# A hybrid prefix-flow block on one core: the softplus of the state space's steps moved ahead of the gated recurrence, two gate panels split ahead of the state space

## The chip, the core and the metric

One Trainium2 chip; the program runs on one of its cores. The time is device microseconds of one execution. Of the kernel before three executions were timed: 3110.61, 3120.03 and 3121.97 us, median 3120.03. A further execution was profiled, and all rows below are of that one.

The engines are named as in the profile: PE is TensorE (PEld its weight loads), DVE is VectorE, ACT is ScalarE, POOL is GpSimd, SP is SyncE, which issues most DMAs.

## The reference, cut to what matters

The block mixes tokens in four branches, gates the branches and sends the result through grouped experts. What this change touches is the fourth branch, a state space (Mamba-like) with a step `dt` per token, direction and head:

```
dt = jax.nn.softplus(dt_raw.reshape(bsz, t_len, 2, H_D) + lp['ssm_dt_bias'])
log_a = dt * (-jnp.exp(lp['ssm_A_log']))[:, None, :, None]
y_f, s_mf = chunk_scan(ch, bh * dt[0][..., None], xh, log_a[0][..., None], s_mf)
y_r, s_mb = chunk_scan(flip_t(ch), flip_t(bh * dt[1][..., None]), flip_t(xh), flip_t(log_a[1][..., None]), s_mb)
...
gates = jax.nn.sigmoid(gate_raw.reshape(bsz, t_len, N_BRANCH, D_MODEL))
merged = gates[:, :, 0] * (branches[0] @ lp['w_branch'][0])
```

The second branch is a gated recurrence (hgrn) over 2048 tokens plus 256 of context, in both directions. The gates are 32 column panels of 128, a matrix product of all tokens with a 1024 x 4096 part of `w_in`.

## The kernel before, in words

All large products run as three float32r products: a weight panel of 128 x 1024 is loaded (`wraw`), cast by ACT to its rounded part (`whi`, L1294), and the rest (`wlo`) is found by a subtraction on DVE or POOL (L1295); this is what "split" means. `wpanel` (L1428) does it, `fetch` (L1420) issues the load. The tokens' rounded part and rest are kept in SBUF (`hb0h`, `hb0l`, `hb1h`, `hb1l`), and `mm3` (L1434) issues the three products (L1438 to L1440) for each of 8 slices of 128, 24 matmuls of 128x512 for one block of 512 tokens.

The order of the program: the projections that hgrn needs for the second half of the tokens (`hgrn_cols(1)`, L1555: four f panels, `token_major` for V and dt_raw, and the panels q0, q1, g0, g1); `hgrn` (L28); the other projections of that half (`other_cols(1)`, L1557); the state space (`ssm`, L182); a convolution branch; a Fourier branch (`fft`); then the gates (L1593), two blocks of tokens for each panel, whose results go to DRAM (`GS`, L1598); then the branch products.

The engines do not follow that order. A scheduler of the framework lays down, before the run, one queue for each engine: an instruction that is ready goes first if it is earlier in the program, and later ones fill the gaps. On the chip each queue is then served in that order. Tiles of one tag are handed out in program order, as their buffers come free; a pool that is opened later uses the memory of one that was closed, and its tiles wait until the older tiles there are done with. Three consequences for what follows:

- PE's gate products fill the gaps of hgrn, of the state space and of the Fourier branch. They go panel by panel, in program order, with 3 PSUM buffers of tag "mm".
- Every third panel (2, 5, 8, ...) keeps its `whi` and `wlo` in the pool `wx` (one buffer), which lies in memory that hgrn's last tiles hold; the others use the ring `wring` (two buffers each). All `wraw` loads share two buffers. Before the change an odd panel's subtraction runs on POOL, an even one's on DVE; the loads of these panels are issued from the POOL queue.
- The first part of the state space (pool `sd`, L193) lies partly in hgrn's memory. So it starts when hgrn ends, though its input dt_raw (`dtr`, written at L1465) is complete long before.

Hgrn (L28) first passes over all tokens for the states (`state_pass`, L72: long runs of small DVE instructions, L85 and L42), then, for each of 4 segments and 2 pairs of heads, goes through 7 levels (L128 to L147: a copy on ACT, 16 matmuls, L137, two masked copies and two products on DVE), and ends with a norm: square on ACT (L168), a matmul (L170), square root on ACT (L172), then on DVE reciprocal (L173), product (L174) and the result `hy` (L176).

The state space (L182) takes the softplus of `dtr` plus its bias (L201 to L214): Exp on ACT (L204), a reciprocal, and a polynomial in a loop of 8 (L211, L212), on DVE, each instruction on 128 x 144 values. It is computed without a Ln. Then `na` = -exp(A_log) (L216, L217), `la` = dt * na (L219), transposes of `la` on PE (L229), ten copies to `R` (L230), a scan over 16 places for each direction (L234), sums over blocks (L241 to L250), Exp on ACT (L251, L252), transposes back (L269). In its second part come the convolution (L279 to L300: three DVE instructions, L289 to L291, for each piece) and the scans over chunks.

Of the kernel before, what the change touches and what calls it, by code (L numbers as in the profile page):

```python
# [4 lines left out]
F32 = mybir.dt.float32  # L5
# [3 lines left out]
AF = mybir.ActivationFunctionType  # L9
OP = mybir.AluOpType  # L10
# [168 lines left out]

def ssm(G, tc, dtr, XR, ZT, XC, XB, cumD, ecumD, elD, SBd, YT):  # L182


    nc = tc.nc
    NCH = TA // 64
    with tc.tile_pool(reuse_waits="tile", name="sst", bufs=1) as st:

        dtm = st.tile([128, 18, 8], F32, name="dtm")
        cumc = st.tile([128, 18, 4, 4], F32, name="cumc")  # L190
        dtw = st.tile([128, 18, 8], F32, name="dtw")
        elB = st.tile([128, NCH, 4], F32, name="elB")
        with tc.tile_pool(reuse_waits="tile", name="sd", bufs=1) as dp:  # L193
            f = [128, 18, 8]
            x = dp.tile(f, F32, name="dx")
            u = dp.tile(f, F32, name="du")
            s = dp.tile(f, F32, name="ds_")
            s2 = dp.tile(f, F32, name="ds2")
            ac = dp.tile(f, F32, name="dac")
            bc = lambda t: t.unsqueeze(1).to_broadcast(f)  # L200
            nc.vector.tensor_tensor(x, dtr, bc(G.dtb), op=OP.add)  # L201
            nc.vector.tensor_scalar(u, x, -1.0, None, op0=OP.mult)
            nc.vector.tensor_tensor(u, u, x, op=OP.min)
            nc.scalar.activation(u, u, AF.Exp)  # L204
            nc.vector.tensor_scalar(s, u, 2.0, None, op0=OP.add)
            nc.vector.reciprocal(s, s)
            nc.vector.tensor_mul(s, s, u)
            nc.vector.tensor_mul(s2, s, s)
            nc.vector.tensor_scalar(ac, s2, 2.0 / 19, 2.0 / 17, op0=OP.mult, op1=OP.add)
            for k in (15, 13, 11, 9, 7, 5, 3, 1):  # L210
                nc.vector.tensor_mul(ac, ac, s2)  # L211
                nc.vector.tensor_scalar(ac, ac, 2.0 / k, None, op0=OP.add)  # L212
            nc.vector.tensor_mul(ac, ac, s)
            nc.vector.scalar_tensor_tensor(dtm, x, 0.0, ac, op0=OP.max, op1=OP.add)  # L214
            na = dp.tile([128, 8], F32, name="na")
            nc.scalar.activation(na, G.alog, AF.Exp)  # L216
            nc.vector.tensor_scalar(na, na, -1.0, None, op0=OP.mult)  # L217
            la = dp.tile(f, F32, name="la")
            nc.vector.tensor_tensor(la, dtm, bc(na), op=OP.mult)  # L219
            R = dp.tile([128, TA], F32, name="R")  # L220
            E = dp.tile([128, TA], F32, name="E")
            nc.gpsimd.memset(R, 0.0)
            for d in range(2):
                p0 = 32 * d
                for i0 in range(0, 18, 4):
                    k = min(4, 18 - i0)
                    pt = G.psum("tr")
                    for i in range(k):
                        nc.tensor.transpose(pt[0:4, i * 128:i * 128 + 128], la[:, i0 + i, d * 4:d * 4 + 4], G.ident)  # L229
                    nc.vector.tensor_copy(R[p0:p0 + 4, i0 * 128:(i0 + k) * 128], pt[0:4, :k * 128])  # L230
                r = R[p0:p0 + 4].rearrange("p (b j) -> p b j", j=16)
                for j in range(1, 16):
                    a, b = (j, j - 1) if d == 0 else (15 - j, 16 - j)
                    nc.vector.tensor_add(r[:, :, a], r[:, :, a], r[:, :, b])  # L234
                rc = R[p0:p0 + 4].rearrange("p (c b j) -> p c b j", b=4, j=16)
                ex = dp.tile([128, NCH, 3], F32, name="ex", bufs=2)
                e = ex[p0:p0 + 4]
                lastj = 15 if d == 0 else 0
                blk = (0, 1, 2) if d == 0 else (3, 2, 1)
                pos = (0, 1, 2) if d == 0 else (2, 1, 0)  # L240
                nc.vector.tensor_copy(e[:, :, pos[0]], rc[:, :, blk[0], lastj])  # L241
                for i in (1, 2):
                    nc.vector.tensor_add(e[:, :, pos[i]], e[:, :, pos[i - 1]], rc[:, :, blk[i], lastj])
                o = 1 - d
                nc.vector.tensor_add(rc[:, :, o:o + 3, :], rc[:, :, o:o + 3, :],
                                     e.unsqueeze(3).to_broadcast([4, NCH, 3, 16]))
                ch = R[p0:p0 + 4].rearrange("p (c j) -> p c j", j=64)
                last = ch[:, :, 63 if d == 0 else 0]
                w = R[p0 + 64:p0 + 68].rearrange("p (c j) -> p c j", j=64)
                nc.vector.tensor_tensor(w, last.unsqueeze(2).to_broadcast([4, NCH, 64]), ch, op=OP.subtract)  # L250
                nc.scalar.activation(R[p0 + 64:p0 + 68], R[p0 + 64:p0 + 68], AF.Exp)  # L251
                nc.scalar.activation(E[p0:p0 + 4], R[p0:p0 + 4], AF.Exp)  # L252
                el = dp.tile([128, NCH], F32, name="el", bufs=2)
                nc.vector.tensor_copy(el[p0:p0 + 4], E[p0:p0 + 4].rearrange("p (c j) -> p c j", j=64)
                                      [:, :, 63 if d == 0 else 0])
                for c2 in range(2):
                    nc.sync.dma_start(cumD[c2, d * 4:d * 4 + 4], ch.rearrange("p (i c) j -> p i c j", c=2)[:, :, c2])
                nc.sync.dma_start(ecumD[d * 4:d * 4 + 4], E[p0:p0 + 4])
                nc.sync.dma_start(elD[d * 4:d * 4 + 4], el[p0:p0 + 4])
                lb = elD[d * 4:d * 4 + 4]  # L260
                elt = dp.tile([128, 4, NCH], F32, name="elt")
                nc.sync.dma_start(elt[d * 64:d * 64 + 64],
                                  bass.AP(tensor=lb.tensor, offset=lb.offset, ap=[[0, 64], [NCH, 4], [1, NCH]]))
                nc.vector.tensor_copy(elB[d * 64:d * 64 + 64], elt[d * 64:d * 64 + 64].rearrange("p h c -> p c h"))
            for i0 in range(0, 18, 4):
                k = min(4, 18 - i0)
                pt = G.psum("tr")
                for i in range(k):
                    nc.tensor.transpose(pt[:, i * 128:i * 128 + 128], R[:, (i0 + i) * 128:(i0 + i + 1) * 128], G.ident)  # L269
                nc.vector.tensor_copy(cumc[:, i0:i0 + k], pt[:, :k * 128].rearrange("p (i q x) -> p i q x", q=4, x=32)  # L270
                                      [:, :, :, 0:4])
            nc.vector.tensor_mul(dtw, dtm, cumc[:, :, 2:4, :].rearrange("p i q h -> p i (q h)"))

        with tc.tile_pool(reuse_waits="tile", name="sw", bufs=1) as wp, tc.tile_pool(reuse_waits="tile", name="ssp", bufs=2) as sp:
# [90 lines left out]
            for sg in range(4):  # L365
# [37 lines left out]
                for i, g in product(range(4), range(2)):  # L403
                    r, s = slice(g * 64, g * 64 + 64), slice(i * 128, i * 128 + 128)
# [8 lines left out]
                for i in range(4):  # L413
# [13 lines left out]
                    for h in range(4):  # L427
                        p, o = at(h)
                        nc.tensor.matmul(p[o, i * 128:i * 128 + 128], xb[:, i, h * 64:h * 64 + 64], PT[:, h, i],
                                         start=True, stop=False)  # L430
                    for c2, h in product(range(2), range(4)):
                        p, o = at(h)
# [792 lines left out]
def build(tc, A, out, dbg=None, stop=99):  # L1225
    nc = tc.nc
    G = G_()
# [48 lines left out]
    QT, GT, ZT = dt_("Q", [2, 128, T]), dt_("G", [2, 128, T]), dt_("Z", [2, 128, T])  # L1276
    XR = dt_("XR", [4, 128, TA])
# [4 lines left out]
    XC = dt_("XC", [4, 128, TA])  # L1282
# [145 lines left out]
    def wpanel(src, pool=None, q=nc.sync, eng=nc.vector):  # L1428
        hi, lo = ((pool or wring).tile([128, 1024], F32R, name=n, bufs=1 if pool else 2) for n in ("whi", "wlo"))
        v = lambda t: t.rearrange("p (k n) -> p k n", n=128)  # L1430
        fetch(v(src), v(hi), v(lo), q, eng=eng)
        return hi, lo
# [70 lines left out]
    def hgrn_cols(half, wt_):  # L1503
        for n in TP[:4]:
            t_panel(n, half)
        token_major(wt_, A["wi"], 264, toks(half), ev_i)
        for n in ("q0", "q1", "g0", "g1"):
            t_panel(n, half)
# [44 lines left out]
    dl = lambda t: [[t[d, p] for p in range(2)] for d in range(2)]  # L1553
    with tc.tile_pool(reuse_waits="tile", name="wtm", bufs=1) as wt_:
        hgrn_cols(1, wt_)  # L1555
        hgrn(G, tc, A["khm"], dl(FT), dl(KT), [QT[0], QT[1]], [GT[0], GT[1]], V, [YT[1, 0], YT[1, 1]], bufs=2)
        other_cols(1, wt_)  # L1557
    wxs = ExitStack()
    wx = wxs.enter_context(tc.tile_pool(reuse_waits="tile", name="wx", bufs=1, side="right"))
    ssm(G, tc, dtr, XR, ZT, XC, XB, cumD, ecumD, elD, SBd, [YT[3, 0], YT[3, 1]])  # L1560
    with tc.tile_pool(reuse_waits="tile", name="bra", bufs=2) as wp:
        for t0 in range(0, T, 512):
# [29 lines left out]

    for js, bs in ((range(24), (0, 1)), (range(24, 32), (0,)), (range(24, 32), (1,))):  # L1593
        for j in js:
            w = wpanel(A["wg"][j], wx if j % 3 == 2 else None, q=nc.gpsimd if len(bs) == 2 else nc.sync, 
                       eng=nc.gpsimd if j % 2 and len(bs) == 2 else nc.vector)
            for b in bs:
                nc.sync.dma_start(GS[b, j], gate(w, T // 2 + b * 512))  # L1598
# [63 lines left out]
```

## Time and profile before

| what | value |
|---|---|
| timed runs | 3110.61, 3120.03, 3121.97 us; median 3120.03 |
| profiled execution | 3115.34 us, its span 3113.5 us |
| PE busy | 2822.9 us, 91% of the span |
| DVE busy | 1839.2 us, 59% |
| ACT busy | 1154.0 us, 37% |
| POOL busy | 574.3 us, 18% |
| mean granted clock of PE | 0.958 |

The span runs from the first to the last instruction; the profiled time holds 1.8 us more. An engine is busy while one of its instructions runs. "Idle before" in a row is the time for which the engine stood still just before that instruction, with the instruction that ended the wait behind the arrow. The granted clock is the share of full speed that PE's clock had, 1.0 or 0.5 at any moment.

### The profile page before, as it was taken

What the parts mean: (1) busy time and instruction counts of PE and PEld (TensorE: products, weight loads), DVE (VectorE), ACT (ScalarE), POOL (GpSimd) and SP (SyncE); (2) the same over time, 40 slices, a digit from 0 to 9 for tenths busy, and PEclk for the clock granted to TensorE, in tenths of its full rate; (3) what the DMA queues carried; (4) which work ended last, traced back from release to release, by engine and by line L of the source; (5) the groups of instructions that cost most, each with busy time, mean ns of one, the idle gap of its engine ahead of it and who ended that gap; (6) DMA issues with size and microseconds to landing.
All of it is one profiled execution on the core that took longest, in us unless ns stands there. A gap on an engine that the chain in (4) does not pass through costs nothing. (4 is left out here: it accounts for less than half of the span.)

```text
span 3113.5 us, 43212 instructions
## 1 busy us (share of the span) xinstructions
PE 2822.9 (91%) x15893; PEld 2229.4 (72%) x15893; DVE 1839.2 (59%) x2870; ACT 1154.0 (37%) x1722; POOL 574.3 (18%) x522
## 2 busy tenths in 40 slices
PE   7999999999967999899999999999688999999992
PEld 3887887787755677777777777887466767776671
DVE  4625125978776478523335333566588777787674
ACT  5411122322336133132222222322366566666552
POOL 3300010000004121013334333100211222111211
PEclk8999999999978899999999999999799999999996
DMA  7736254423118476866335433655698889998786
GB/s 288 252 111 214 80 166 146 155 86 95 68 43 267 130 213 195 268 230 236 122 125 181 160 115 133 195 177 162 198 331 296 287 291 299 307 319 289 251 270 232
DMA packets 245981, 621.46 MB, mean 200 GB/s; under 512 B 31128, under 2 KB 81464, under 8 KB 242008
## 3 DMA queue, kind: packets, MB, share of 16 engines
q1 hardware_dynamic: 211312, 506.17, 46.9%
q0 software_dynamic: 34416, 111.88, 12.8%
q8 instruction: 163, 2.67, 0.3%
q14 instruction: 90, 0.74, 0.1%
HBM read 484.86 MB, written 137.28 MB: 200 GB/s over the span
## 5 line engine op out<-in xcount | busy, mean ns | idle before, releaser
L1295 DVE TENSOR_TENSOR mlo<-mraw,mhi 128x1024 fp32r<-128x1024 f32 x382 | 450.2, 1225 | 58.5 <-ACT mhi L1294 53.0
L1294 ACT CAST mhi<-mraw 128x1024 fp32r<-128x1024 f32 x384 | 383.6, 1047 | 84.3 <-issue 44.7
L1438 PE MATMUL ps_mm<-hb1h,wlo 128*128 128x512 f32 x800 | 320.0, 400 | 3.7 <-DVE wlo L1295 3.7
L1440 PE MATMUL ps_mm<-hb1h,whi 128*128 128x512 f32 x800 | 318.3, 398 | 0.0
L1439 PE MATMUL ps_mm<-hb1l,whi 128*128 128x512 f32 x800 | 318.3, 398 | 0.0
L1589 ACT ACTIVATE ev<-ps_mm 128x512 f32<-128x512 f32 x128 | 76.2, 597 | 618.5 <-PE ps_mm L1440 515.6
L1295 DVE TENSOR_TENSOR wlo<-wraw,whi 128x1024 fp32r<-128x1024 f32 x164 | 217.2, 1333 | 142.6 <-ACT whi L1294 142.4
L1438 PE MATMUL ps_mm<-hb0h,wlo 128*128 128x512 f32 x672 | 269.5, 401 | 16.0 <-DVE wlo L1295 12.5
L1439 PE MATMUL ps_mm<-hb0l,whi 128*128 128x512 f32 x672 | 269.7, 401 | 0.0
L1440 PE MATMUL ps_mm<-hb0h,whi 128*128 128x512 f32 x672 | 267.8, 398 | 0.0
L1294 ACT CAST whi<-wraw 128x1024 fp32r<-128x1024 f32 x176 | 182.2, 1045 | 163.8 <-PE ps_mm L1440 70.0
L1438 PE MATMUL ps_mm<-mhi,xl 128*128 128x512 f32 x512 | 205.7, 402 | 24.5 <-PEq L956 24.2
L1639 POOL TENSOR_TENSOR macc<-macc,ev 128x512 f32<-128x512 f32 x96 | 167.1, 1740 | 307.0 <-DVE ev L1638 304.0
L1638 DVE TENSOR_TENSOR ev<-ev,ps_tr 128x512 f32<-128x512 f32 x96 | 65.8, 687 | 248.7 <-PE ps_tr L1440 243.8
L1439 PE MATMUL ps_mm<-mlo,xh 128*128 128x512 f32 x512 | 202.4, 395 | 3.2 <-ACT mhi L1294 2.4
L1440 PE MATMUL ps_mm<-mhi,xh 128*128 128x512 f32 x512 | 201.8, 394 | 1.4 <-issue 1.4
L1438 PEld LDWEIGHTS ps_mm<-hb1h,wlo 128*128 128x128 f32 x800 | 151.5, 189 | 38.2 <-DVE wlo L1295 4.1
L1440 PEld LDWEIGHTS ps_mm<-hb1h,whi 128*128 128x128 f32 x800 | 151.3, 189 | 33.1 <-issue 2.4
L1439 PEld LDWEIGHTS ps_mm<-hb1l,whi 128*128 128x128 f32 x800 | 151.4, 189 | 32.4 <-issue 1.9
L1438 PEld LDWEIGHTS ps_mm<-hb0h,wlo 128*128 128x128 f32 x672 | 127.7, 190 | 45.7 <-DVE wlo L1295 14.1
L869 POOL DMA_INDIRECT xg<-d_FR,idx x48 | 67.5, 1406 | 459.4 <-ACT w L904 444.1
L1439 PEld LDWEIGHTS ps_mm<-hb0l,whi 128*128 128x128 f32 x672 | 127.9, 190 | 29.5 <-issue 3.4
(592 smaller groups left out, 5861.0 us busy)
## 6 DMA issues: line engine op xcount, KB each, us to landing
mraw<-e SPq DMA_DIRECT2D x372, 512.0 KB
wraw<-wg SPq DMA_DIRECT2D x80, 512.0 KB
wraw<-wt SPq DMA_DIRECT2D x40, 512.0 KB
aw<-adaw SPq DMA_DIRECT2D x64, 256.0 KB
d_GS<-ev SPq DMA_DIRECT2D x64, 256.0 KB
ev<-d_GS POOLq DMA_DIRECT2D x64, 256.0 KB, 4.3
wraw<-wg POOLq DMA_DIRECT2D x24, 512.0 KB, 3.9
d_FR<-hb0h SPq DMA_DIRECT2D x22, 512.0 KB
```

Source lines behind the costliest of these rows:

```text
L869: nc.gpsimd.indirect_dma_start(out=xg, out_offset=None, in_=FR, in_offset=bass.IndirectOffsetOnAxis(ap=idx_ap, axis=0), bounds_check=2 * T ...
L1294: nc.scalar.copy(hi, raw)
L1295: eng.tensor_sub(lo, raw, hi.bitcast(F32))
L1438: nc.tensor.matmul(ps, wl, xh, start=start and n == 0, stop=False)
L1439: nc.tensor.matmul(ps, wh, xl, start=False, stop=False)
L1440: nc.tensor.matmul(ps, wh, xh, start=False, stop=stop and n == len(ks) - 1)
L1589: nc.scalar.activation(g, ps, AF.Sigmoid)
L1638: nc.vector.tensor_mul(g, g, ps)
L1639: nc.gpsimd.tensor_add(acc, acc, g)
```

## The change

The softplus becomes a function `steps` of its own, which writes over `dtr`, in slices of two tiles of tag "ev" (the tag of the panels' results). It is called after `hgrn_cols(1)` and before `hgrn`. `ssm` takes `dtr` as `dtm`; its tile `dtm` and five tiles of pool `sd` fall away. Panels 0 and 1 of the gates are fetched and split before `ssm` in program order, both with the subtraction on DVE; the gate loop takes them from a list.

```
-def ssm(G, tc, dtr, XR, ZT, XC, XB, cumD, ecumD, elD, SBd, YT):
+def steps(G, tc, dtr, tmp):
+
+    nc = tc.nc
+    f = [128, 18, 8]
+    x, u, s, s2, ac = (t[:, k * 144:k * 144 + 144].rearrange("p (i d) -> p i d", d=8) 
+                       for t, n in ((tmp(), 3), (tmp(), 2)) for k in range(n))
+    bc = lambda t: t.unsqueeze(1).to_broadcast(f)
+    nc.vector.tensor_tensor(x, dtr, bc(G.dtb), op=OP.add)
+    nc.vector.tensor_scalar(u, x, -1.0, None, op0=OP.mult)
+    nc.vector.tensor_tensor(u, u, x, op=OP.min)
+    nc.scalar.activation(u, u, AF.Exp)
+    nc.vector.tensor_scalar(s, u, 2.0, None, op0=OP.add)
+    nc.vector.reciprocal(s, s)
+    nc.vector.tensor_mul(s, s, u)
+    nc.vector.tensor_mul(s2, s, s)
+    nc.vector.tensor_scalar(ac, s2, 2.0 / 19, 2.0 / 17, op0=OP.mult, op1=OP.add)
+    for k in (15, 13, 11, 9, 7, 5, 3, 1):
+        nc.vector.tensor_mul(ac, ac, s2)
+        nc.vector.tensor_scalar(ac, ac, 2.0 / k, None, op0=OP.add)
+    nc.vector.tensor_mul(ac, ac, s)
+    nc.vector.scalar_tensor_tensor(dtr, x, 0.0, ac, op0=OP.max, op1=OP.add)
+
+
+def ssm(G, tc, dtm, XR, ZT, XC, XB, cumD, ecumD, elD, SBd, YT):
...
-        dtm = st.tile([128, 18, 8], F32, name="dtm")
...
-            f = [128, 18, 8]
-            x = dp.tile(f, F32, name="dx")
...
-            nc.vector.tensor_mul(ac, ac, s)
-            nc.vector.scalar_tensor_tensor(dtm, x, 0.0, ac, op0=OP.max, op1=OP.add)
             na = dp.tile([128, 8], F32, name="na")
             nc.scalar.activation(na, G.alog, AF.Exp)
             nc.vector.tensor_scalar(na, na, -1.0, None, op0=OP.mult)
...
         hgrn_cols(1, wt_)
+        steps(G, tc, dtr, lambda: ev.tile([128, 512], F32, name="ev", tag="ev", bufs=4))
         hgrn(G, tc, A["khm"], dl(FT), dl(KT), [QT[0], QT[1]], [GT[0], GT[1]], V, [YT[1, 0], YT[1, 1]], bufs=2)
         other_cols(1, wt_)
     wxs = ExitStack()
     wx = wxs.enter_context(tc.tile_pool(reuse_waits="tile", name="wx", bufs=1, side="right"))
+    ahead = [wpanel(A["wg"][j], q=nc.gpsimd, eng=nc.vector) for j in range(2)]
     ssm(G, tc, dtr, XR, ZT, XC, XB, cumD, ecumD, elD, SBd, [YT[3, 0], YT[3, 1]])
...
         for j in js:
-            w = wpanel(A["wg"][j], wx if j % 3 == 2 else None, q=nc.gpsimd if len(bs) == 2 else nc.sync, 
+            w = ahead.pop(0) if ahead else wpanel(A["wg"][j], wx if j % 3 == 2 else None, q=nc.gpsimd if len(bs) == 2 else nc.sync, 
                        eng=nc.gpsimd if j % 2 and len(bs) == 2 else nc.vector)
```

## Rows read from the trace of the kernel before

**Rows 1.** The page's first part: busy time, share and instructions of each engine.

```profile
PE 2822.9 (91%) x15893; PEld 2229.4 (72%) x15893; DVE 1839.2 (59%) x2870; ACT 1154.0 (37%) x1722; POOL 574.3 (18%) x522
```

**Rows 2.** Busy time by stretch: PE, PEld, DVE, ACT, POOL; granted clock, DMA share, GB/s.

```profile
505.00:600.00 95.00, 87.34 (x516) 68.51 (x516) 88.67 (x265) 23.23 (x37) 0.00 (x0) 1.00 0.57 186
600.00:849.00 249.00, 239.22 (x1856) 192.02 (x1855) 198.75 (x321) 76.59 (x119) 9.45 (x8) 1.00 0.26 84
849.00:893.00 44.00, 22.34 (x130) 17.72 (x128) 25.68 (x58) 11.75 (x15) 2.54 (x2) 0.55 0.13 42
940.00:1050.00 110.00, 89.16 (x363) 65.07 (x362) 62.56 (x85) 46.85 (x64) 35.93 (x47) 0.81 0.72 228
1050.00:1280.00 230.00, 227.75 (x1367) 170.06 (x1366) 171.56 (x233) 61.37 (x75) 36.80 (x30) 1.00 0.67 200
```

**Rows 3.** The stores of the gates' results (L1598): issue min/median/max ns, first to last.

```profile
L1598 SPq DMA_DIRECT2D d_GS<-ev x64: 319/332/1566, 818.9 to 1430.5; - x64
```

**Rows 4.** PE's waits, 849 to 1050 us: total us, times, longest.

```profile
PE ps_mm L1438 <- DVE wlo L1295: 12.5, 1, 12.5
PE ps_tr L297 <- ACT cy L292: 11.1, 3, 5.8
PE ps_tr L269 <- issue: 8.1, 1, 8.1
```

**Rows 5.** Timeline of ACT at the turn: start us, duration us, instruction, idle before.

```profile
881.87 1.28 ACT L204 ACT_TABLE_LOAD   x1
...
887.60 1.04 ACT L1294 CAST whi<-wraw 128x1024 fp32r<-128x1024 f32 x1 [4.11 <-DVE hy L176]
```

**Rows 6.** Timeline of DVE at the turn, 868 to 900 us.

```profile
868.33 0.30 DVE L201 TENSOR_TENSOR dx<-dtr,c_dtb 128x144 f32<-128x144 f32 x1
...
879.89 0.17 DVE L217 TENSOR_SCALAR na<-na 128x8 f32<-128x8 f32 x1 [10.65 <-ACT na L216]
881.89 3.35 DVE L173 RECIPROCAL rr<-rr 128x512 f32<-128x512 f32 x1 [1.83 <-ACT rr L172]
...
886.91 0.65 DVE L176 SCALAR_TENSOR_TENSOR hy<-rr,c_hnw,hg 128x512 f32<-128x512 f32 x1
...
891.72 1.22 DVE L1295 TENSOR_TENSOR wlo<-wraw,whi 128x1024 fp32r<-128x1024 f32 x1
...
896.50 0.31 DVE L219 TENSOR_TENSOR la<-dtm,na 128x144 f32<-128x144 f32 x1
...
898.87 1.27 DVE L230 COPY R<-ps_tr 4x512 f32<-4x512 f32 x2
```

**Rows 7.** Groups of DVE, 868 to 897 us: count, busy us, mean ns, idle before.

```profile
L211 DVE TENSOR_TENSOR dac<-dac,ds 128x144 f32<-128x144 f32 x8 | 2.5, 307 | 0.2
L212 DVE TENSOR_SCALAR dac<-dac 128x144 f32<-128x144 f32 x8 | 1.9, 232 | 0.2
...
L206 DVE RECIPROCAL ds__7044<-ds__7044 128x144 f32<-128x144 f32 x1 | 1.0, 1047 | 0.0
```

**Rows 8.** Timelines of ACT and DVE where the moved softplus would start.

```profile
503.85 0.60 ACT L1491 ACTIVATE ev<-ps_mm 128x512 f32<-128x512 f32 x1 [4.85 <-PE ps_mm L1440]
...
505.51 0.48 DVE L66 COPY SF<-ps_tr 64x64 f32<-64x64 f32 x2 [9.76 <-PE ps_tr L60]
```

**Rows 9.** Timelines of POOL and DVE while POOL splits panel 1, and after.

```profile
807.21 2.47 POOL L1295 TENSOR_TENSOR wlo<-wraw,whi 128x1024 fp32r<-128x1024 f32 x1 [24.31 <-ACT whi L1294]
...
807.36 2.40 DVE L42 TENSOR_TENSOR tot<-tot 128x64 f32<-128x64 f32 x1
...
812.11 0.18 DVE L42 TENSOR_TENSOR tot<-tot 128x32 f32<-128x32 f32 x1
```

**Rows 10.** Groups of DVE, 898.5 to 917 us.

```profile
L234 DVE TENSOR_TENSOR R<-R 4x144 f32<-4x144 f32 x26 | 11.0, 423 | 0.8
L230 DVE COPY R<-ps_tr 4x512 f32<-4x512 f32 (+1 forms) x10 | 5.9, 622 | 0.2
```

**Rows 11.** Group of PE, 879 to 1050 us.

```profile
L229 PE MATMUL ps_tr<-c_kid,la 128*4 128x128 f32 x36 | 5.5, 290 | 0.5 <-DVE R L230 0.4
```

More of the change, by code (lines that the diff above doesn't have):

```diff
@@ L193, in ssm @@
         with tc.tile_pool(reuse_waits="tile", name="sd", bufs=1) as dp:
-            f = [128, 18, 8]
-            x = dp.tile(f, F32, name="dx")
[L196 to L212, printed above, removed]
-            nc.vector.tensor_mul(ac, ac, s)
-            nc.vector.scalar_tensor_tensor(dtm, x, 0.0, ac, op0=OP.max, op1=OP.add)
             na = dp.tile([128, 8], F32, name="na")
@@ L217, in ssm @@
             nc.vector.tensor_scalar(na, na, -1.0, None, op0=OP.mult)
-            la = dp.tile(f, F32, name="la")
-            nc.vector.tensor_tensor(la, dtm, bc(na), op=OP.mult)
+            la = dp.tile([128, 18, 8], F32, name="la")
+            nc.vector.tensor_tensor(la, dtm, na.unsqueeze(1).to_broadcast([128, 18, 8]), op=OP.mult)
             R = dp.tile([128, TA], F32, name="R")
```

## The prediction, made before the change ran

> **What bounds the kernel.** I read first the page's totals: TensorE (PE) is busy for 2822.9 of 3113.5 us [rows 1]. Then I read busy time by stretch, to see where the missing 291 us lie [rows 2]. From 505 to 600 us VectorE (DVE) is nearly full (88.7 of 95) and PE has little room; from 600 to 849 PE is the full one (239.2 of 249). Then comes the turn from the gated recurrence (hgrn) to the state space: from 849 to 893 PE is busy for 22.3 of 44 us at a mean granted clock of 0.55, the lower level being 1.2 of 2.4 GHz. From 940 to 1050 it loses another 21 us, at 0.81. From 1050 to 1280 it is full again.
>
> Third, I asked whether the state space's own length sets the end. The gate panels are PE's filler, and their results are stored from 818.9 to 1430.5 us [rows 3], long after the state space has gone. So PE never runs out of gate work, and **the time is PE's work plus PE's idle stretches**: a shorter state-space chain is worth only what it takes out of PE's idle time. The waits list names that [rows 4]: 12.5 us at once for the split of a gate panel (wlo), 11.1 us for the state space's convolution, 8.1 us before the transposes of L269 (their releaser isn't named; what they read is the decay table R, last written by ScalarE).
>
> The 12.5 us are the heart of it. The panel is panel 2, whose tiles lie in pool wx, in memory that hgrn's last tiles hold. Its cast waits for hgrn's last DVE instruction, hy, and starts at 887.60 [rows 5]; its subtraction starts at 891.72, 4.2 us after hy ended (886.91 and 0.65), in a gap that the softplus left, in which each instruction waits for the one before it [rows 6]. Gates take panels in program order, so PE waits for this one.
>
> **The change, part by part.**
>
> *The softplus leaves the turn.* It is 26 DVE instructions: 8 multiplies for 2.5 us, 8 additions for 1.9, a reciprocal for 1.0 [rows 7], and nine more of 0.2 to 0.3 like the first [rows 6], 2.5 in all: 7.8 us, with one Exp and a table load of 1.28 on ScalarE [rows 5]; no DMA. Now its result la comes at 896.50; what la needs besides, na, starts its last step at 879.89 [rows 6]. So la can come about 16 us sooner after hgrn's end. Two of its instructions, the reciprocal and a small addition, also stand between hgrn's last ones: hy comes 1.2 us sooner.
>
> *It lands in hgrn's first part.* Its five vectors lie in two "ev" tiles, which are handed out in program order, behind those of panel g1; the last of these is filled at 503.85 on ScalarE [rows 8]. DVE stands idle just before 505.51 [rows 8], so three instructions fit there, and the Exp with its load lies beside DVE work. The other 23 (7.0 us) meet a DVE that has 6.3 us free in 95 [rows 2]. They are ahead of hgrn in program order and so in priority: hgrn's state passes, queued behind them, wait. Hgrn's length from 505 us to the turn hangs on DVE and on latency, and PE's filler inside it is fixed (panels 0 and 1 are the last that fit). So a delay of hgrn becomes PE idle time at the turn. Bounds: 0, if later idle DVE time (50 us between 600 and 849) takes it up, and 8. I take 6, near the upper end, as that idle time comes in waits within a chain. While the softplus runs, "ev" has two tiles instead of four for xs0's results; PE has three PSUM buffers ahead of that, so nothing.
>
> *Panels 0 and 1 ahead.* This half hardly moves anything: panel 1 is already split at 807.21 [rows 9], and panel 0 before it, since the state space can't start sooner than hgrn's memory comes free. Their DMAs stay on the POOL queue in the same order, behind the same buffers. What changes is panel 1's engine: 1.22 us on DVE (the duration in [rows 6]) instead of 2.47 us on POOL. While POOL split it, a DVE multiply (L42) that reads two SBUF tiles took 2.40 us; a like one of half its width took 0.18 [rows 9]. So the move costs DVE 1.2 and gives back 2.2: hgrn gains 1.0 us. The Trainium skill (GPSIMD Engine Reference, Specifications) says that GpSimd's SBUF interfaces are shared with VectorE and contend when a VectorE instruction has two SBUF inputs; the stretched L42 agrees. Counted without that rule, the move would cost hgrn 1.2 us and the sum would be 2.2 higher.
>
> *Panel 2's split gets new neighbours.* With la early, the ten copies into R (5.9 us) and the scan over sixteen places (26 of its 30 instructions here, 11.0 us) fall where the softplus was [rows 10]. In the profile these run almost without a gap from 898.87: two scans alternate, so neither leaves a gap for work of lower priority. Panel 2's split has lower priority than everything in the state space, and is ready some 1.2 us after hy. Two or three copies fit before hy, since hgrn's own reciprocal of 3.35 us [rows 6] stands there; some 15 us remain. Bounds: no later than now (4.2 us after hy) if it slips in among the copies, and 25 later if the convolution's instructions take the first gaps after the scans as well. I take **13 later** (start 17 us after hy: right behind the scans), which is nearest to the row of the scans.
>
> *What PE gets back.* The 36 transposes of la (5.5 us [rows 11]) now fall into PE's idle stretch instead of beside gates: 5.5 less (bounds 0 and 5.5; I take all, as they are ready before the split is). The 8.1 us before L269 [rows 4] arise because gate work queued ahead had run out before ScalarE's Exp of R ended; with the chain sooner and the gates later, PE has more to do then. Bounds 0 and 8.1; I take 4. The 21 us between 940 and 1050 I leave as they are: they hang on convolution, loads and latency, which the change doesn't touch.
>
> **Sum:** hgrn later 6 - 1.0 = 5.0; hy sooner -1.2; split later +13; transposes -5.5; L269 -4: **+7.3 us**. The profiled execution took 3115.3 us (span 3113.5 and 1.8 around it), 4.7 below the median of 3120.0. By its own time that is 3122.6, from the median 3127.
>
> **Rivals.** *Slower: the split falls behind the convolution too.* After the scans the context's convolution has nine DVE instructions waiting, ahead of the split in priority. If they take the gaps, the split is 25 us later and gates wait in PE's queue so long that L269 is no stall of its own but gives nothing back either: 7 - 1 - 1.2 + 25 - 5.5 = +24, 3144 us. It decides once the split starts later than about 20 us after hy. For it: in [rows 10] the scans let nothing in. Against it: the tail of the scans is a chain with gaps.
>
> *Faster: the split finds a gap as now, and the earlier chain empties PE's stalls.* Then +5.0 - 1.2 + 0 - 2 (part of the transposes) - 8.1, and half of the 21 us between 940 and 1050, since convolution and state scan come some 10 us sooner while gates are not later: -17, 3103 us. For it: two of the three largest waits in [rows 4] are on the state space's chain. Against it: a chain's shift moves such a stall as easily as it removes it.
>
> *Nothing reaches PE.* The split finds its gap, the stalls only shift: 5.0 - 1.2 - 3 = +1, 3121 us. The second half of the change does nothing in every case.
>
> **How the numbers follow.** Forecast 0.34, slower rival 0.26, faster rival 0.26, nothing 0.14. The forecast's own range is 3115 to 3138. A measurement of this kernel tells about 0.5% (15.6 us) from no change. Slower by more: four fifths of the slower rival and an eighth of the forecast, 0.25, and 0.02 for an order that turns out worse elsewhere. Faster: four fifths of the faster rival and 0.03 of the rest, 0.24. Same: 0.49. The range runs from 3099 (a little beyond the faster rival) to 3149 (beyond the slower one); it leaves out about 0.1 at either end, the parts of the two rivals beyond their own sums.
>
> **What would show it.** Right: the softplus multiplies at 505 to 520 us; hgrn's hy some 4 us later than 886.91; la within 4 us of na; panel 2's subtraction right behind the scans' last instruction; PE idle for 20 us or more, instead of 12.5, between hgrn's last matmul and panel 2's first gate, transposes apart; the wait before L269 shorter. Wrong: 12 us or less there (the split slipped in), hy not later (DVE had room), or PE's idle time from 940 to 1050 changed by more than 10 us, which would be the order of the state space, not the turn.

## The result, and the profile after

The changed kernel takes 3142.35 us (median of 12 runs, 3132.95 to 3151.36), the kernel before, beside it, 3122.39 (12 runs). The ratio is 1.0072, 95% interval 1.0055 to 1.0089: some 22.5 us (17 to 28) slower. The two medians alone lie 20.0 us apart (1.0064), inside that interval; what follows goes by the ratio, which is not that of the medians. The time is inside the range of 3099 to 3149, but the ratio is beyond the 0.5% that the prediction could not tell from no change, on the side that it gave a chance of 0.27; the forecast was 3127, and the slower rival stood at 3144. The profiled execution took 3143.49 us, span 3141.7. The lines of the state space and of the helpers stand 1 lower in the listing than before (L269 is now L270, L229 is L230, L1295 is L1296), those of the gates 3 lower; `steps` is L182 to L202.

First, PE's waits in the changed kernel, 849 to 1050 us (columns as in [rows 4]):

```profile
PE ps_mm L1439 <- DVE wlo L1296: 28.5, 1, 28.5
PE ps_sc L137 <- DVE QP L143: 11.9, 5, 2.9
PE ps_tr L298 <- ACT cy L293: 5.5, 3, 2.4
```

The wait for panel 2's split has grown from 12.5 to 28.5 us. The 8.1 us before L269 of [rows 4] are gone, those for the convolution's result have halved.

Second, busy time by stretch (columns as in [rows 2]), first of the kernel before, for two stretches that [rows 2] leaves out:

```profile
893.00:920.00 27.00, 26.47 (x122) 20.17 (x123) 24.69 (x62) 6.29 (x8) 2.29 (x4) 0.91 0.21 69
920.00:940.00 20.00, 11.93 (x60) 10.24 (x59) 14.73 (x26) 16.82 (x13) 1.08 (x2) 0.83 0.26 75
```

and of the changed kernel:

```profile
893.00:920.00 27.00, 8.47 (x37) 3.87 (x36) 24.54 (x50) 2.91 (x4) 0.00 (x0) 0.56 0.13 39
920.00:940.00 20.00, 7.05 (x31) 6.26 (x32) 14.56 (x30) 15.63 (x11) 1.63 (x3) 0.54 0.23 69
940.00:1050.00 110.00, 98.19 (x415) 73.59 (x413) 58.58 (x85) 54.61 (x72) 35.58 (x48) 0.90 0.72 228
```

From 893 to 920 PE is busy for 8.5 us instead of 26.5, nearly all of it the transposes of la, and the granted clock is at its lower level up to 940 (hgrn ends 13.3 us later than in the kernel before, which is part of this). DVE is as busy as before: it is the engine that everybody waits for. Part of the loss comes back after 940 (98.2 instead of 89.2 us).

Third, DVE's timeline at the turn, to be read beside [rows 6]:

```profile
893.01 0.31 DVE L220 TENSOR_TENSOR la<-dtr,na 128x144 f32<-128x144 f32 x1
894.58 0.68 DVE L231 COPY R<-ps_tr 4x512 f32<-4x512 f32 x1 [1.26 <-PE ps_tr L230]
895.19 3.33 DVE L173 RECIPROCAL rr<-rr 128x512 f32<-128x512 f32 x1
...
900.18 0.73 DVE L176 SCALAR_TENSOR_TENSOR hy<-rr,c_hnw,hg 128x512 f32<-128x512 f32 x1
900.85 1.71 DVE L231 COPY R<-ps_tr 4x512 f32<-4x512 f32 x3
...
906.85 9.21 DVE L235 TENSOR_TENSOR R<-R 4x144 f32<-4x144 f32 x22
916.09 0.19 DVE L242 COPY ex<-R 4x36 f32<-4x36 f32 x1
916.22 0.06 DVE L283 MEMSET xin<- 128x1 f32 x1
...
917.57 0.39 DVE L290 TENSOR_SCALAR cy<-xin,c_scw 128x256 f32<-128x256 f32 x1
917.89 1.94 DVE L246 TENSOR_TENSOR R<-R,ex 4x1728 f32<-4x1728 f32 x1
...
923.28 0.48 DVE L291 SCALAR_TENSOR_TENSOR cy<-xin,c_scw,cy 128x256 f32<-128x256 f32 x1
...
925.93 0.48 DVE L291 SCALAR_TENSOR_TENSOR cy<-xin,c_scw,cy 128x256 f32<-128x256 f32 x1
926.45 1.95 DVE L246 TENSOR_TENSOR R<-R,ex 4x1728 f32<-4x1728 f32 x1
928.43 0.48 DVE L292 SCALAR_TENSOR_TENSOR cy<-xin,c_scw,cy 128x256 f32<-128x256 f32 x1
928.94 2.55 DVE L251 TENSOR_TENSOR R<-R 4x2304 f32<-4x2304 f32 x1
931.56 0.06 DVE L285 MEMSET xin<- 128x1 f32 x1
931.57 0.06 DVE L283 MEMSET xin<- 128x1 f32 x1
931.67 1.22 DVE L1296 TENSOR_TENSOR wlo<-wraw,whi 128x1024 fp32r<-128x1024 f32 x1
```

la comes before hy instead of 9 us behind it. Panel 2's subtraction, which stood 4.2 us behind hy's end, now stands 30.8 us behind it (931.67 less 900.91), though its cast could start at once, as ScalarE's timeline shows:

```profile
900.95 1.04 ACT L1295 CAST whi<-wraw 128x1024 fp32r<-128x1024 f32 x1 [6.17 <-DVE hy L176]
```

Fourth, how much of hy's lateness the recurrence itself made. DVE's timeline at hgrn's first state copy, at its first reciprocal, and while the softplus runs:

```profile
501.25 0.31 DVE L191 TENSOR_TENSOR ev<-ev 128x144 f32<-128x144 f32 x1
510.48 0.47 DVE L66 COPY SF<-ps_tr 64x64 f32<-64x64 f32 x2 [8.93 <-PE ps_tr L60]
...
513.29 0.23 DVE L193 TENSOR_SCALAR ev<-ev 128x144 f32<-128x144 f32 x1
513.43 0.29 DVE L85 TENSOR_TENSOR ks<-ks,tot 128x128 f32<-128x128 f32 x1
513.64 1.05 DVE L194 RECIPROCAL ev<-ev 128x144 f32<-128x144 f32 x1
...
523.65 0.30 DVE L202 SCALAR_TENSOR_TENSOR dtr<-ev 128x144 f32<-128x144 f32 x1
...
622.36 3.35 DVE L173 RECIPROCAL rr<-rr 128x512 f32<-128x512 f32 x1 [0.86 <-ACT rr L172]
```

hy starts at 900.18 instead of 886.91 [rows 6], 13.3 us later. But the first state copy is already 5.0 us later than in [rows 8], and nothing of the softplus but three instructions in idle time stands ahead of it; from one profile to another that start lies anywhere between 505.5 and 512.5. From first state copy to hy it is 389.7 us against 381.4: **hgrn takes 8.3 us longer**. All of it arises by the first reciprocal (111.9 us after the first copy; the kernel before has it at 608.74, 103.2 after). In that stretch DVE has the softplus's 7.0 us more, and one panel split more (7 instead of 6, of 1.2 us each). That the softplus holds two of the "ev" tiles doesn't show there: ScalarE's first copy of a projection's result into one starts 5.4 us after the first state copy, 5.3 in the kernel before.

### The profile page after: what moved, and what is told of

The parts are those of the page before. It is cut to its first block, busy times and chain, and to the rows that moved or that the text cites. A ratio compares the mean times of both kernels' runs of the same rounds, so it can differ in the third digit from the quotient of the medians.

```text
span 3141.7 us, 43225 instructions
## 1 busy us (share of the span) xinstructions
PE 2839.1 (90%) x15893; PEld 2238.1 (71%) x15893; DVE 1835.1 (58%) x2873; ACT 1152.3 (37%) x1719; POOL 572.8 (18%) x521
## 5 line engine op out<-in xcount | busy, mean ns | idle before, releaser
L1296 DVE TENSOR_TENSOR mlo<-mraw,mhi 128x1024 fp32r<-128x1024 f32 x382 | 450.5, 1226 | 59.7 <-ACT mhi L1295 54.4
L1295 ACT CAST mhi<-mraw 128x1024 fp32r<-128x1024 f32 x384 | 384.8, 1047 | 89.7 <-issue 43.4
L1296 DVE TENSOR_TENSOR wlo<-wraw,whi 128x1024 fp32r<-128x1024 f32 x165 | 216.9, 1322 | 140.9 <-ACT whi L1295 140.7
L1439 PE MATMUL ps_mm<-hb0h,wlo 128*128 128x512 f32 x672 | 268.8, 400 | 28.5 <-DVE wlo L1296 28.5
L1295 ACT CAST whi<-wraw 128x1024 fp32r<-128x1024 f32 x176 | 182.0, 1043 | 153.7 <-PE ps_mm L1441 78.4
```

The lines of the kernel that those rows point to most:

```text
L1295: nc.scalar.copy(hi, raw)
L1296: eng.tensor_sub(lo, raw, hi.bitcast(F32))
L1439: nc.tensor.matmul(ps, wl, xh, start=start and n == 0, stop=False)
```

## The experiments

Three theories were put against each other. **S**: the loss is panel 2's split, kept back on DVE by work of higher priority. **H**: the loss is the softplus inside the recurrence, which ends later. **O**: the order of panels 0 and 1 costs the time. Ratios are against the kernel before on the same chip; from chip to chip its own median went from 3118.84 to 3139.96 us, so only ratios are compared, and the us are the ratio's distance from 1 times that median. Each variant was timed 12 times, e1 6 times. In the table "hgrn" is from the first state copy's start to the last hy's, "split" from hy's end to the start of panel 2's subtraction, "gates" from the first state copy to the last store of a gate. These three are from one profile each: e8 and e12 are the same kernel and differ by 1.6 us in hgrn and 6.1 in gates.

| kernel | ratio (95%) | us | hgrn | split | gates |
|---|---|---|---|---|---|
| before | 1 | 0 | 381.4 | 4.2 | 925.0 |
| changed | 1.0072 (1.0055 to 1.0089) | +22.5 | 389.7 | 30.8 | 939.2 |
| e1 softplus alone | 1.0070 (1.0043 to 1.0098) | +21.8 | 388.6 | 30.8 | 939.7 |
| e2 panels 0, 1 alone | 0.9995 (0.9975 to 1.0014) | -1.6 | 379.3 | 4.2 | 921.5 |
| e3 panel 2 ahead too | 1.0010 (0.9992 to 1.0028) | +3.1 | 388.6 | 5.1 | 923.4 |
| e4 softplus earlier | 1.0043 (1.0023 to 1.0062) | +13.4 | 381.1 | 30.8 | 930.7 |
| e5 both | 0.9977 (0.9957 to 0.9997) | -7.2 | 380.7 | 5.1 | 921.2 |
| e6 before, panel 2 ahead | 1.0000 (0.9983 to 1.0017) | 0.0 | 380.6 | 4.2 | 926.6 |
| e7 split on POOL | 0.9997 (0.9980 to 1.0015) | -0.9 | 389.1 | 2.7 | 919.1 |
| e8 both, split on POOL | 0.9966 (0.9949 to 0.9983) | -10.7 | 381.1 | 2.6 | 906.5 |
| e10 panel 2 between | 1.0008 (0.9989 to 1.0028) | +2.5 | 389.0 | 15.3 | 922.4 |
| e11 between, softplus earlier | 0.9966 (0.9946 to 0.9985) | -10.7 | 379.4 | 15.3 | 902.9 |
| e12 as e8 | 0.9978 (0.9957 to 0.9998) | -6.9 | 379.5 | 2.6 | 912.6 |

**e1, the softplus alone.** The list of panels ahead is taken out of the changed kernel.

```diff
-    ahead = [wpanel(A["wg"][j], q=nc.gpsimd, eng=nc.vector) for j in range(2)]
...
-            w = ahead.pop(0) if ahead else wpanel(...)
+            w = wpanel(...)
```

> The changed kernel without its second half: panels 0 and 1 are requested in program order after the state space again, the softplus stays where the change put it. Theory S (the loss is panel 2's split, which waits on DVE behind the copies, scans and convolution of the state space) and theory H (the loss is the softplus's DVE time inside the gated recurrence, which ends later) both expect the second half to do nothing but panel 1's engine: within 6 us of the changed kernel, so some 15 to 25 us above the kernel before, panel 2's subtraction again 25 us or more after hy. Theory O (the order of panels 0 and 1 ahead costs the time, the softplus is harmless) expects the time of the kernel before, within 6 us.

**e2, the second half alone.** The kernel before with that list.

> The second half alone: panels 0 and 1 are requested ahead of the state space, the softplus stays in the state space. Theories S and H: the kernel before within 5 us, panel 2's subtraction 4 us after hy in the softplus's gap. Theory O: 15 us or more above the kernel before.

e1 is as slow as the changed kernel, with the same 30.8 us and the same wait of 28.5 us for the split; e2 can't be told from the kernel before. O falls: the second half does nothing measurable, the softplus's move does it all.

**e3, panel 2 ahead as well.**

```diff
-    ahead = [wpanel(A["wg"][j], q=nc.gpsimd, eng=nc.vector) for j in range(2)]
+    ahead = [wpanel(A["wg"][j], wx if j == 2 else None, q=nc.gpsimd, eng=nc.vector) for j in range(3)]
```

> The changed kernel with panel 2 (the one in hgrn's memory) requested ahead of the state space too, so that its split stands ahead of copies, scans and convolution in priority. Theory S: its subtraction starts 2 to 5 us after hy instead of 30.8, PE has gate work some 26 us sooner, and the time falls by 13 to 22 us against the changed kernel, back to the kernel before within 7 us. Theory H: hgrn still ends as late, and the time is within 6 us of the changed kernel.

**e4, the softplus one place sooner**, its five vectors in the memory of the projection's weights, so that it runs while panels q0 to g1 do.

```diff
         token_major(wt_, A["wi"], 264, toks(half), ev_i)
+        if half:
+            steps(G, tc, dtr, lambda t=wt_.tile([128, 2112], F32, name="stp", tag="tmh"), n=iter((0, 512)): t[:, next(n):])
...
-        steps(G, tc, dtr, lambda: ev.tile([128, 512], F32, name="ev", tag="ev", bufs=4))
```

> The changed kernel with the softplus one place sooner: right behind the projection that gives it its input, ahead of panels q0 to g1, in memory of the projection's weights, where DVE has idle time and no recurrence runs. Theory H: DVE in hgrn's state passes is as before the change, hy comes 7 to 13 us sooner than in the changed kernel, and the time falls by 13 to 20 us. Theory S: hy comes some 8 us sooner and the time falls by at most that, since panel 2's subtraction still starts 25 us or more after hy.

e3 is 19 us faster than the changed kernel (1.0072 less 1.0010) with hgrn as long as there, so S holds for the larger part. e4 has hgrn back at 381.1 us and gains 9 by the ratios (10 between the medians of e1 and e4, on the same chip), about as much as hgrn gave back; the 13 that H expected at least are missed, and 13.4 us remain while the split still comes 30.8 us behind hy. e4 is the price of the late split, less what PE gets back, and the difference to the changed kernel the price of the softplus's place. The longer recurrence is visible in PE's waits too: in the 60 us that end with hy, that for QP (L137) is 11.9 us in the changed kernel, 6.0 in the one before and 5.9 in e4.

**e5, both repairs, and e6, panel 2 ahead in the kernel before.**

> Both repairs together: the softplus behind its projection, and panel 2 requested ahead of the state space. If the split's place and hgrn's delay are two separate costs that add (the repairs gave 19 and 9 us one by one), it runs some 6 us below the kernel before (-2 to -10): hy as long after hgrn's first state copy as before the change (381 us), panel 2's subtraction about 5 us after hy. If the two cover the same PE idle time, the second repair gives nothing and the time stays within 3 us of the kernel before.

> The kernel before, softplus in the state space, with panels 0 to 2 requested ahead of the state space. Theory S (the split was early before because the softplus's chain left a gap for it): priority has almost nothing to give here, the subtraction starts 1 to 4 us after hy instead of 4.2, and the time is within 4 us of the kernel before. If instead a panel in hgrn's memory requested ahead is a gain by itself, whatever the softplus does, the time falls by more than 8 us.

The two costs add: e5 is at -7.2 us. In e6 the split is where it was, 4.2 us behind hy (1 to 4 were expected): with the softplus beside it the gap was free anyway, and priority gives nothing. What the change took away is that gap.

**e7, panel 2's subtraction on POOL**, nothing else changed, and **e8**, the same with both repairs.

```diff
-                       eng=nc.gpsimd if j % 2 and len(bs) == 2 else nc.vector)
+                       eng=nc.gpsimd if (j % 2 or j == 2) and len(bs) == 2 else nc.vector)
```

> The changed kernel with panel 2's subtraction on POOL instead of DVE, nothing else moved. Theory S in its narrow form (only DVE's queue holds the split back): the subtraction starts within 3 us after the cast of panel 2, takes some 2.5 us and stretches DVE instructions beside it by 1 to 3 us; the time falls by 12 to 20 us against the changed kernel. If the cast or the panel's place in the order is what is late, the subtraction still starts 20 us or more after hy and the time stays within 5 us of the changed kernel.

> Both repairs, and panel 2's subtraction on POOL besides. It starts about 2 us after hy instead of 5 and takes 2.5 us instead of 1.2, so panel 2's gate comes some 2 us sooner, against 1 to 3 us of stretched DVE work in the copies and scans: within 4 us of the version with both repairs and the subtraction on DVE.

POOL's timeline in e7, then DVE's beside it:

```profile
900.97 2.33 POOL L1296 TENSOR_TENSOR wlo<-wraw,whi 128x1024 fp32r<-128x1024 f32 x1 [19.41 <-DMA xin<-d_XR]
```

```profile
900.33 0.68 DVE L231 COPY R<-ps_tr 4x512 f32<-4x512 f32 x1
901.04 2.52 DVE L235 TENSOR_TENSOR R<-R 4x144 f32<-4x144 f32 x1
903.59 0.68 DVE L231 COPY R<-ps_tr 4x512 f32<-4x512 f32 x1
```

The cast ends at 899.31, POOL starts 1.7 us later and takes 2.33 us; one addition of DVE is held for it, 2.52 us instead of 0.39. For these 2.1 us of DVE, e7 is 23 us faster than the changed kernel, somewhat more than the 12 to 20 expected, so nothing but DVE's queue held the split. e8 is 3.5 us below e5, within the 4 expected; the intervals don't tell the two apart.

**e9 and e10, panel 2 requested inside the state space**, behind the decay chain and ahead of the convolution; e9 is a single execution, e10 the same kernel timed 12 times. By then I held that the rest of the decay chain (L246 and L251, twice, 9.0 us together), not the convolution (2.8 us by my count then), had kept the split back.

```diff
             nc.vector.tensor_mul(dtw, dtm, cumc[:, :, 2:4, :].rearrange("p i q h -> p i (q h)"))
+        between()
...
+        lambda: ahead.append(wpanel(A["wg"][2], wx, q=nc.gpsimd, eng=nc.vector)))
```

> The changed kernel with panel 2 requested inside the state space, behind the decay chain's last multiply and ahead of the convolution, so that in priority its split stands behind copies and scans but ahead of every instruction of the convolution. If the convolution is what kept the split 30.8 us behind hy (as the slower rival of the prediction had it), it now starts 15 to 20 us after hy, right behind the scans over sixteen places. If the rest of the decay chain (the long additions and subtractions over all places, 9.0 us) is what held it, the split gains only the convolution's share, 2.8 us, and starts 27 to 30 us after hy; PE's wait for it stays above 23 us.

> The same kernel as the look before (panel 2 requested between the decay chain and the convolution), timed. There the split started 15.3 us after hy, close to the 17 that the prediction took, with the long additions and subtractions of the decay chain behind it: the convolution's instructions, ahead of the split in priority, had taken those gaps. If the prediction's sum for a split at that place holds, the time is 3 to 11 us above the kernel before (its sum was 7.3); if a split that comes this late costs nothing more than the idle time that the transposes and the wait before L269 fill anyway, it is within 3 us of the kernel before or below it. In both cases it is 10 us or more below the changed kernel.

e9's single time is 3133.9 us beside 3134.27 of the kernel before, and its split starts 15.3 us behind hy: my theory fell. DVE's timeline of e10, where it starts at the same distance (these lines stand 1 lower again from the convolution on, L1297 is L1296):

```profile
904.68 9.24 DVE L235 TENSOR_TENSOR R<-R 4x144 f32<-4x144 f32 x22
913.95 0.19 DVE L242 COPY ex<-R 4x36 f32<-4x36 f32 x1
914.07 1.21 DVE L1297 TENSOR_TENSOR wlo<-wraw,whi 128x1024 fp32r<-128x1024 f32 x1
915.20 0.20 DVE L244 TENSOR_TENSOR ex<-ex,R 4x36 f32<-4x36 f32 x1
...
916.58 1.95 DVE L246 TENSOR_TENSOR R<-R,ex 4x1728 f32<-4x1728 f32 x1
919.01 2.55 DVE L251 TENSOR_TENSOR R<-R 4x2304 f32<-4x2304 f32 x1
...
922.17 0.41 DVE L291 TENSOR_SCALAR cy<-xin,c_scw 128x256 f32<-128x256 f32 x1
```

The chain does open a slot, right behind the paired additions. In e10 the split takes it. In the changed kernel, at the same place (916.09 to 917.57), it is the convolution's small instructions that are let in, and theirs are the next slots too. So 3.1 us of convolution (six products of 0.4 to 0.5 us and seven short fills between 916 and 931.7), ahead of the split in priority, put it off by 15.5 us, since each slot is given out once. The change from e10 to the changed kernel costs 20 us by the ratios (1.0072 less 1.0008). e10's own +2.5 us (-3.5 to 8.8) doesn't tell its two expectations apart. PE's side of it, e10's busy time by stretch:

```profile
893.00:920.00 27.00, 11.98 (x43) 7.24 (x44) 25.80 (x49) 2.44 (x3) 0.53 (x1) 0.56 0.18 59
920.00:940.00 20.00, 19.30 (x94) 15.73 (x94) 12.31 (x29) 16.98 (x14) 3.49 (x3) 0.99 0.28 83
```

From 920 PE is full at the upper clock, and the wait before L270 is 0.7 us. The wait for the split is 12.8 us, hardly more than the 12.5 of [rows 4], though the split comes 11.2 us later behind hy: in between PE does the transposes of la (8.3 us) and waits for copies among them (3.0).

**e11, e10 with the softplus one place sooner, and e12, e8 once more beside it.**

> As the run before, with the softplus behind its projection instead of ahead of the gated recurrence. hgrn's delay is gone (hy 381 us after its first state copy), so 8 to 9 us less than the run before: 3 to 12 us below the kernel before.

> The version with the softplus behind its projection, panel 2 requested ahead of the state space and its subtraction on POOL, beside the two others on one chip: 0.3% below the kernel before again (6 to 15 us), and within 5 us of the version that requests panel 2 between decay chain and convolution, which has its split some 12 us later but ahead of the same transposes.

Both beat the kernel before and the changed one, by 10.7 and 6.9 us against the former; they can't be told from each other, 12.7 us of difference in the split's place notwithstanding. e11 is 13 us below e10 where 8 to 9 were expected; the intervals allow both.

## Why the prediction failed in its forecast and held in a rival

*The mechanism was right:* the time is PE's work and its idle time at the turn; the softplus's chain had made the gap for panel 2; the change takes it away and fills DVE with copies and scans. The softplus does run at 500 to 524 us, la does come right behind na (0.2 us), PE is idle for 28.5 us, the wait before L269 is gone. It was the slower rival that happened, in its place and by its engine: the split fell behind the convolution, later than the 20 us behind hy from which the rival was said to decide.

*The step that failed* is "I take 13 later (start 17 us after hy: right behind the scans)". The first slot does lie there (15.3 us, e10), so the row was read rightly; but the same text said that the convolution's nine instructions wait ahead of the split in priority, and did not give them the slot. Measured: 26.6 us later. Against the rival I wrote that the tail of the scans is a chain with gaps; gaps are no help to the last in the queue.

*The other terms, with their sizes.* hgrn later: 6 less 1.0 predicted, 8.3 measured, just above the upper bound of 8. The 7.0 us of 23 instructions are not taken up by later idle time, and DVE waits somewhat more as well (for L115's transposes 3.3 us instead of 2.0 until the first reciprocal). Panel 1's gain of 1.0 can't be told from these profiles: without the second half, in e1, hgrn is 1.1 us shorter rather than longer, and with the second half alone, in e2, 2.1 shorter than before, but the same kernel twice (e8, e12) differs by 1.6. "hy comes 1.2 us sooner": nothing, for the copies into R take the place that the softplus leaves there (reciprocal to hy 4.99 us, before 5.02). The wait before L269: 4 of 8.1 predicted, all 8.1 gone; the rival was wrong to give back nothing. Transposes: 5.5, as taken, all in the idle stretch.

With the measured sizes the sum is 8.3 + 26.6 - 5.5 - 8.1 = +21.3 us, against +22.5 measured (17 to 28). The same sum for e4 (-0.3 + 26.6 - 5.5 - 8.1) is +12.7 against 13.4, for e10 (7.6 + 11.2 - 5.5 - 7.4) +5.9 against 2.5. That the rival's +24 (3144) lies so near is in part luck, for its errors partly cancel: hgrn's delay 3.5 us and the split's 1.6 too small, against 8.1 us before L269 that it did not give back. These sums take hgrn and the split from one profile each.

*The second half does nothing* was right (e2, -1.6 us; 1 and 21.8 with e1). The window from 940 to 1050, which I left as it was, gained 9 us of busy PE, just inside the 10 that I had set as a sign of being wrong.

*Left open.* The sum is an account by terms and no full ledger: for e11 the terms (-2.0 + 11.2 - 5.5 - 6.4) give -2.7 us, and it measures -10.7 (-17 to -5); where the other 8 us come from was not settled. For e8 they give -5.2 (hgrn -0.3, the split's end -0.5, the transposes of la -5.5, which lie ahead of panel 2's first gate there too, 9.2 us before L270 instead of 8.1); it measures -10.7 and in e12, the same kernel, -6.9. And of the 28.2 us between the two profiled spans only 14.2 lie between first state copy and last gate store; 5.0 lie ahead, 9 behind, where nothing was changed and single executions differ by as much.

## What to carry to other kernels

Before taking a chain of dependent work out of a full stage, look who used its gaps: here a 1.22 us split on which PE waited lived in them. Work that another engine waits for has to be requested ahead of work that nobody waits for yet, for on a full engine the last in priority gets not the first gap but the last; its price is read from the time at which every instruction ahead of it has had its slot. And work moved into a stage whose engine is 93% busy cost its whole length there; one place sooner, where the engine idles, it cost nothing. Nor is every delay paid for: the cost of a split 15.3 us behind hy (e10, e11) could not be told from that of one 5.1 or 2.6 us behind (e3, e5, e12), as the transposes filled part of PE's wait; at 30.8 it cost some 20 us.

## What the runs showed of the hardware

A DVE addition with both inputs in SBUF (two places of the tile R) ended 0.26 us after POOL's subtraction ended, both in e7 (901.04 and 2.52 against 900.97 and 2.33) and in e8 (894.28 and 2.37 against 894.05 and 2.34), though alone it takes 0.39: it looks like being shut out until POOL is done, not like sharing. The Trainium skill (SBUF — State Buffer, Summary: rules for kernel authors) says that where VectorE has two SBUF inputs while GpSimd reads SBUF, the second to issue fully blocks until the first has finished; both runs agree.

PE's 36 small transposes of la cost 8.1 us in the idle stretch (granted clock 0.56 there), 5.5 among the gates [rows 11]; the 18 of R cost 404 ns each in the changed kernel and 274 in e10, where gates run just ahead of them. By line, of the changed kernel:

```profile
L230 PE MATMUL ps_tr<-c_kid,la 128*4 128x128 f32 x36 | 8.1, 406 | 3.0 <-DVE R L231 2.9
L270 PE MATMUL ps_tr<-c_kid,R 128*128 128x128 f32 x18 | 3.8, 404 | 0.0
```

and of e10:

```profile
L270 PE MATMUL ps_tr<-c_kid,R 128*128 128x128 f32 x18 | 2.2, 274 | 0.7 <-issue 0.7
```

The granted clock while the transposes of R ran was 0.54 in the changed kernel, just behind the 28.5 us wait, and 1.00 in e10. A late gate panel so costs its wait and slower transposes around it besides. But an early one doesn't spare them: in e8 PE stands idle for 9.2 us just ahead of the transposes of R, and they run at 0.50 and take 424 ns each. In these runs it is PE's idle time just before that goes with the lower clock, whatever caused it.
